# First projections on x times the norm's gains, the reciprocal root applied behind them

## The chip, the core and the metric

The kernel runs on one core of a Trainium2 chip. The metric is the device time of one execution in microseconds (us), with all data in the chip's memory at the start and the result there at the end. Of several runs the median is taken.

Five engines take part, each working through its own instructions in order: TensorE (PE in the profile, with its weight loads as PEld), VectorE (DVE), ScalarE (ACT), GpSimd (POOL) and SyncE (SP), which issues most of the DMAs. They wait for each other through semaphores only.

## The reference

The program is a two-layer encoder trunk over 256 tokens of 1024 values. The start of a layer, which is all that the change touches, is this (shortened):

```python
def rms_norm(x, g):
    y = x * rsqrt(mean(x * x, axis=-1) + 1e-6)
    return y * g

u = rms_norm(h, g_mix_pre)            # h is x in layer 0
z = u @ w_in                          # one wide projection, cut into:
#  GLA q | GLA k | GLA v | out-gate gg | decay ranks | GQA q | GQA k | GQA v | gate A | gate B
# GQA: q and k get a per-head RMSNorm (eps 1e-6) and rotary positions, then attention
# GLA: gated linear attention over chunks with decays made from the ranks; gates by sigmoids
# then merge, output projection, residual; SwiGLU FFN; per-layer input embedding
```

The reciprocal root is one number per token, so `(x * g) @ w` scaled by it afterwards is the same function.

## The kernel before

**Precision.** Every fp32 product is made of three passes over values rounded for TensorE. An operand t is split into a high part (ACT copies it to the rounded type) and a low part (DVE subtracts the high part from t). The three passes are high times high, low of x times high of the weights, high of x times low of the weights. In the names, `wh_` and `wl_` are the weights' parts, `raw_` the weights as loaded, `big_start` (uT in the code) the transposed x.

**Staging.** Tokens are two halves, hf 0 and hf 1, of 128. Weights come in units through a stream `ws`: a unit is a DMA of about 1 MB into one of a few raw tiles, two casts on ACT and two subtractions on DVE (`ws.pieces()` hands out the two pieces). The projections follow one another on PE: rq (the decay ranks and GQA's q, columns cut in three by `RQ`, 288, 384 and 384 wide), kv (GQA's k and v), gqk (GLA's q and k), v, gg, then the gates. Rq takes four units of two 128-row blocks each; its order is written out in `STEPS_FIRST` (half 0 and half 1 of unit 0, then of unit 1, and so on), with 6 accumulators of PSUM, one for each half and column block. `rq_first` writes out unit 0 pass by pass.

**Order by hand at the start.** `on(engine, f, ...)` (line 142) chains what is issued through it on its engine in the order in which the program says it; `start()` is a generator that says it, and the projection advances it by `tick()`. In the generator: squares of a half (`square` on ACT, `square_here` on DVE), the reciprocal root on POOL (`rstd`), `normed` (DVE multiplies x by the root), `turned` (PE transposes 128x128 blocks; gains applied on the way out of PSUM while splitting, column by column, or for four columns at once by one DVE multiplication of 512 columns ahead of the split). `warm_up(n)` issues matmuls on constants into a PSUM tile that nobody reads; `WARM` gives their numbers at three places. `grow` is the row of gains as loaded, `gcol` the same turned to a column by `gains()`.

**Behind the projections.** `put_q` (lines around 940) takes each accumulator of rq when its last unit is done: for the first column block `put_ranks` copies the decay ranks (POOL memsets a tile, three DVE copies), then `head_ss` squares each head on ACT with its sum, `inv_sqrt` makes the reciprocal roots on POOL in two instructions, and `rope` multiplies on DVE. `keys` does the same for kv. Behind gqk ACT copies four accumulators of 128x512 (lines 1124 and 1126). Where `tc.high_priority` stands, the scheduler moves the instructions ahead in their queues; `EMPTY_FIRST`, 1600, is the amount for layer 0's `put_q`, `EMPTY`, 100, for `keys`.

```python
with tc.high_priority(EMPTY if l else EMPTY_FIRST):
    if b == 0:
        ranks.append(Task(put_ranks(o, hf), part[0]))
    ...
    head_ss(src, n, dst, ss[:, hd : hd + n])
    inv_sqrt(ss[:, hd : hd + n], n, 1.0, P * EPS)
    rope(src, n, ropes[0], hf, dst)
```

## Time and profile before

| what | value |
|---|---|
| runs of before | 923.92, 924.27, 924.66 us |
| median | 924.27 us |
| span of the profiled execution | 922.9 us |
| median less that span | 1.4 us |
| PE busy | 912.2 us, 99% of the span |
| DVE busy | 786.1 us, 85% |
| ACT busy | 578.5 us, 63% |
| POOL busy | 83.8 us, 9% |
| first product of rq, of kv, of gqk | 7.92, 36.43, 47.56 us |

The profiled execution has no time of its own beside its span; the span runs from the first to the last instruction, and 1.4 us lie around it when it is set against the median. In the rows of the timeline the columns are start, length, engine, line, operation, output and inputs, shape, and how many instructions the row stands for; in brackets stands how long the engine idled before and what ended the wait. Lines that several instructions go through (120 and 104 for matmuls, 128 and 132 for splits, 142 for all of the start) are helpers: there the names of the tiles tell the rows apart. In the chain of waits the columns are start, length and what; "issue" is time in which the engine waited for nothing that the profile shows.

### The profile page before, as it was taken

Reading aid. Unit: us, or ns where it says so; the run is one execution under the profiler, and the core shown is the slowest. Engines: PE = TensorE matmul, PEld = TensorE weight load, DVE = VectorE, ACT = ScalarE, POOL = GpSimd, SP = SyncE. Lnnn points to the kernel's source line nnn. Section 1 sums busy time; section 2 is a strip of 40 time slices with the busy share of each in tenths; the row PEclk is TensorE's granted clock in tenths of the full one; section 3 lists DMA queues with packets and bytes.
Section 4 is the critical chain, followed back from the end, with each engine's and each line's share of the span. In section 5 each row is a group of like instructions: output and inputs, shape, how many; then the busy total and the mean of one; then the engine's idle time right before and its main releaser. Section 6 shows DMA issues by size and latency. Waiting matters only on the chain.

```text
span 922.9 us, 12406 instructions
## 1 busy us (share of the span) xinstructions
PE 912.2 (99%) x4668; PEld 776.2 (84%) x4668; DVE 786.1 (85%) x1002; ACT 578.5 (63%) x954; POOL 83.8 (9%) x147
## 2 busy tenths in 40 slices
PE   9999999999999999999999999999999999999996
PEld 6898888888888888888899988888888888888885
DVE  6898989987579998999779789798875799989884
ACT  4669676664567656566676677765644766565563
POOL 3400211300000000000114001100001000000000
PEclk9999999999999999999999999999999999999999
DMA  7463455656286565647576424454573756545361
GB/s 260 144 230 134 148 173 188 201 193 232 90 277 222 178 233 168 265 128 268 188 256 220 153 92 137 137 191 174 195 260 104 268 177 204 223 177 217 126 239 45
DMA packets 88679, 173.44 MB, mean 188 GB/s; under 512 B 3422, under 2 KB 26470, under 8 KB 88108
## 3 DMA queue, kind: packets, MB, share of 16 engines
q1 hardware_dynamic: 88460, 172.40, 54.0%
q8 instruction: 36, 0.59, 0.3%
q10 hardware_dynamic: 160, 0.27, 0.1%
q14 instruction: 23, 0.19, 0.1%
HBM read 169.50 MB, written 3.15 MB: 187 GB/s over the span
## 4 chain that ended last, share of the span: by engine, by line
PE 94%; DVE 2%; ACT 1%; DMA 1%; issue 1%; POOL 0%; POOLq 0%; DVEq 0%; ACTq 0%; SPq 0%
PE acc_0ffnin L120 12%; PE acc_1ffnin L120 11%; PE acc_1gate L120 7%; PE acc_0gate L120 7%; PE acc_0ffnin L104 7%; PE acc_1ffnin L104 7%; PE acc_1rq L120 3%; PE acc_0gqk L120 2%; PE acc_0wout L120 2%; PE acc_1gqk L120 2%; PE acc_1ple L120 2%; PE acc_0ple L120 2%; PE acc_0gg L120 2%; PE acc_1gg L120 2%; PE acc_0v L120 2%; PE acc_1merge L120 2%
## 5 line engine op out<-in xcount | busy, mean ns | idle before, releaser
L104 PE MATMUL acc_0ffnin<-wh_0ffnin,big_0ffnin 128*128 128x512 f32 x176 | 56.9, 393 | 0.0
L104 PE MATMUL acc_1ffnin<-wh_1ffnin,big_1ffnin 128*128 128x512 f32 x176 | 56.8, 392 | 0.0
L132 ACT CAST wh_1ffnin<-raw_1ffnin 128x1024 fp32r<-128x1024 f32 x38 | 38.5, 1049 | 27.3 <-DMA raw_1ffnin<-in_w_ffn_out_dram 8.7
L132 ACT CAST wh_0ffnin<-raw_0ffnin 128x1024 fp32r<-128x1024 f32 x38 | 38.4, 1048 | 23.8 <-PE acc_0ffnin L120 7.8
L128 DVE TENSOR_TENSOR wl_1ffnin<-raw_1ffnin,wh_1ffnin 128x1024 fp32r<-128x1024 f32 x38 | 45.0, 1221 | 8.9 <-ACT wh_1ffnin L132 8.9
L128 DVE TENSOR_TENSOR wl_0ffnin<-raw_0ffnin,wh_0ffnin 128x1024 fp32r<-128x1024 f32 x38 | 44.8, 1220 | 7.1 <-ACT wh_0ffnin L132 7.0
L120 PE MATMUL acc_1ffnin<-wh_1ffnin,big_1wout 128*128 128x512 f32 x168 | 42.5, 393 | 0.0
L120 PE MATMUL acc_0ffnin<-wh_0ffnin,big_0wout 128*128 128x512 f32 x168 | 42.5, 393 | 0.0
L104 PEld LDWEIGHTS acc_0ffnin<-wh_0ffnin,big_0ffnin 128*128 128x128 f32 x176 | 33.0, 188 | 7.1 <-DVE big_0ffnin L128 0.5
L104 PEld LDWEIGHTS acc_1ffnin<-wh_1ffnin,big_1ffnin 128*128 128x128 f32 x176 | 33.1, 188 | 6.7
L128 DVE TENSOR_TENSOR wl_1ffnin<-lent_1ffnin,wh_1ffnin 128x1024 fp32r<-128x1024 f32 x30 | 35.8, 1218 | 1.7 <-ACT wh_1ffnin L132 1.7
L128 DVE TENSOR_TENSOR wl_0ffnin<-lent_0ffnin,wh_0ffnin 128x1024 fp32r<-128x1024 f32 x30 | 35.8, 1216 | 1.7 <-ACT wh_0ffnin L132 1.7
L120 PEld LDWEIGHTS acc_1ffnin<-wh_1ffnin,big_1wout 128*128 128x128 f32 x168 | 31.1, 188 | 6.2
L120 PEld LDWEIGHTS acc_0ffnin<-wh_0ffnin,big_0wout 128*128 128x128 f32 x168 | 31.1, 188 | 6.2
L132 ACT CAST wh_1ffnin<-lent_1ffnin 128x1024 fp32r<-128x1024 f32 x30 | 30.7, 1053 | 7.1 <-PE acc_1ffnin L104 3.9
L132 ACT CAST wh_0ffnin<-lent_0ffnin 128x1024 fp32r<-128x1024 f32 x30 | 30.7, 1054 | 6.7 <-PE acc_0ffnin L104 3.9
L104 PE MATMUL acc_0ffnin<-wl_0ffnin,big_0ffnin 128*128 128x512 f32 x88 | 34.3, 389 | 0.0
L104 PE MATMUL acc_1ffnin<-wl_1ffnin,big_1ffnin 128*128 128x512 f32 x88 | 34.3, 389 | 0.0
L128 DVE TENSOR_TENSOR wl_1gate<-raw_1gate,wh_1gate 128x1024 fp32r<-128x1024 f32 x20 | 23.6, 1219 | 5.4 <-ACT wh_1gate L132 5.3
L128 DVE TENSOR_TENSOR wl_0gate<-raw_0gate,wh_0gate 128x1024 fp32r<-128x1024 f32 x20 | 23.7, 1226 | 4.8 <-ACT wh_0gate L132 4.8
L132 ACT CAST wh_0gate<-raw_0gate 128x1024 fp32r<-128x1024 f32 x20 | 20.0, 1048 | 11.7 <-DMA raw_0gate<-in_w_o_attn_dram 5.6
L132 ACT CAST wh_1gate<-raw_1gate 128x1024 fp32r<-128x1024 f32 x20 | 20.0, 1049 | 11.5 <-DMA raw_1gate<-in_w_o_attn_dram 5.5
(695 smaller groups left out, 2691.8 us busy)
## 6 DMA issues: line engine op xcount, KB each, us to landing
raw_0ffnin<-in_w_ffn_out_dram SPq DMA_DIRECT2D x11, 1024.0 KB, 6.6
raw_1ffnin<-in_w_ffn_out_dram SPq DMA_DIRECT2D x11, 1024.0 KB, 5.1
lent_0ffnin<-in_w_ffn_in_dram SPq DMA_DIRECT2D x6, 1024.0 KB, 7.4
lent_1ffnin<-in_w_ffn_in_dram SPq DMA_DIRECT2D x6, 1024.0 KB, 8.3
raw_0v<-in_w_in_dram SPq DMA_DIRECT2D x4, 1024.0 KB, 4.9
raw_0gate<-in_w_o_gla_dram SPq DMA_DIRECT2D x4, 1024.0 KB, 4.9
raw_0gate<-in_w_o_attn_dram SPq DMA_DIRECT2D x4, 1024.0 KB, 5.1
raw_0wout<-in_w_ffn_in_dram SPq DMA_DIRECT2D x8, 512.0 KB, 4.9
```

Of the source, the lines that this page charges most:

```text
L104: return nc.tensor.matmul(o, lhsT, rhs, start=start, stop=stop)
L120: nc.tensor.matmul(o, x, y, start=start and n == 0, stop=stop and n == len(seq) - 1, **kw)
L128: nc.vector.tensor_tensor(out=out, in0=in0, in1=in1, op=ALU.subtract)
L132: nc.scalar.copy(hi, src)
```

## The change

Norm and projection change places in layer 0. x is transposed as it lands; its gains are applied during the split, its reciprocal root `rs` behind each projection: as the scale of the squares in `head_ss`, as one more POOL multiplication behind `inv_sqrt`'s two instructions (`by`), in `put_ranks`, in the splits of v and of the values of kv (`split_by`), in the copies of gg and in the sigmoids of the gates. Gqk's accumulators have tokens along the free axis, so the roots are needed as a row there: `spread_rows` makes it (two diagonals on DVE, two matmuls against ones on PE, one ACT copy), emitted right behind the keys, and the four evictions of gqk move from ACT to DVE, which multiplies by that row.

The left 512 columns of both halves are loaded first, each on a queue of its own; the right columns follow the first weights. `rq_first` takes both halves' blocks in turn. The squares and roots move behind unit 1, the rotary tables (`rope_tables`) into `start()`, ahead of the decay's weights (`up_weights`). The warming matmuls become 6 of 128 columns (on `seed`, written by POOL), 6 and 3 of 512 columns. Unchanged lines are mostly left out, and the body of the removed `turned`.

```diff
--- before.py
+++ after.py
...
 RQ = ((0, 288), (288, 672), (672, 1056))
-WARM = 7, 3, 1
+WARM = 6, 6, 3
...
             line[e] = f(*args, **kw)
+    seed = cp.tile([P, P], BF16, tag="seed", name="seed")
+    on("pool", nc.gpsimd.memset, seed, 1.0)
...
     grow = mid()[0:8, 0:P]
-    def load_x(hf, queues=(("dma", nc.sync), ("dma", nc.sync))):
-        for j, (e, q) in enumerate(queues):
-            c = slice(j * 512, (j + 1) * 512)
-            on(e, q.dma_start, h[:, hf, c], a["x"][0, hf * P : (hf + 1) * P, c])
-    load_x(0, (("dma", nc.sync), ("act", nc.scalar)))
+    def load_x(hf, j, e="dma", q=nc.sync):
+        c = slice(j * 512, (j + 1) * 512)
+        on(e, q.dma_start, h[:, hf, c], a["x"][0, hf * P : (hf + 1) * P, c])
+    load_x(0, 0)
+    load_x(1, 0, "act", nc.scalar)
+    on("act", nc.scalar.dma_start, grow, a["g_mix_pre"][0].rearrange("(k p) -> k p", p=P))
...
         return tc.issue_after(last_pow[0].ins) if last_pow[0] is not None else nullcontext()
-    def inv_sqrt(t, n, mul, add):
+    def inv_sqrt(t, n, mul, add, by=None):
...
         last_pow[0] = nc.gpsimd.tensor_tensor(out=t, in0=t, in1=neghalf[:, :n], op=ALU.pow)
+        if by is not None:
+            with in_turn():
+                last_pow[0] = nc.gpsimd.tensor_scalar(out=t, in0=t, scalar1=by, scalar2=None, op0=ALU.mult)
+    def split_by(hi, lo, src, r):
+        if r is None:
+            return split(hi, lo, src)
+        nc.scalar.activation(hi, src, AF.Copy, bias=0.0, scale=r)
+        nc.vector.scalar_tensor_tensor(
+            out=lo, in0=src, scalar=r, in1=hi.bitcast(F32), op0=ALU.mult, op1=ALU.subtract
+        )
...
         return wup
-    x1 = [lambda: load_x(1)]
-    on("act", nc.scalar.dma_start, grow, a["g_mix_pre"][0].rearrange("(k p) -> k p", p=P))
-    ws.load(lambda: x1 and x1.pop()())
     ws.load()
+    ws.load()
+    load_x(0, 1)
+    load_x(1, 1)
...
     gcol = small(8, "gcol", 1)
-    def warm_up(n):
+    def warm_up(n, wide=False):
+        x = keep if wide else seed
         for _ in range(n):
-            on("pe", mm, warm, keep[:, 0:P], keep, True, True)
+            on("pe", mm, warm[:, 0 : x.shape[-1]], seed, x, True, True)
     warm_up(WARM[0])
+    warm_up(WARM[1], True)
     uT = Split()
-    ss, rs, xn = [small(2, "ss") for _ in range(2)], [small(1, "rstd") for _ in range(2)], [mid(), mid()]
+    ss = [small(2, "ss") for _ in range(2)]
+    rs, ropes_first = [small(1, "rs", 2) for _ in range(2)], []
...
         last_pow[0] = line["pool"]
-    def normed(hf, k, n):
-        c = slice(k * P, (k + n) * P)
-        on("dve", nc.vector.tensor_scalar, out=xn[hf][:, c], in0=h[:, hf, c], scalar1=rs[hf], scalar2=None, op0=ALU.mult)
     def gains():
...
         on("dve", nc.vector.tensor_copy, gcol, ps[:, 0:8])
+    def low(hi, lo, src):
+        on("dve", nc.vector.tensor_tensor, out=lo, in0=src, in1=hi.bitcast(F32), op=ALU.subtract)
     def split_here(hi, lo, src):
         on("act", nc.scalar.copy, hi, src)
-        on("dve", nc.vector.tensor_tensor, out=lo, in0=src, in1=hi.bitcast(F32), op=ALU.subtract)
-    def turned(hf, k, n):
...
+        low(hi, lo, src)
+    banks = {}
+    def turn(hf, *ks):
+        if (hf, ks[0] // 4) not in banks:
+            banks[hf, ks[0] // 4] = aux()
+        for k in ks:
+            ps = banks[hf, k // 4][:, k % 4 * P : (k % 4 + 1) * P]
+            on("pe", nc.tensor.transpose, ps, h[:, hf, k * P : (k + 1) * P], ident)
+    def high(hf, *ks):
+        for k in ks:
+            ps = banks[hf, k // 4][:, k % 4 * P : (k % 4 + 1) * P]
+            on("act", nc.scalar.activation, uT.at(k, 1, hf * P, P)[0][:, 0, :], ps, AF.Copy, bias=0.0, scale=gcol[:, k : k + 1])
+    def rest(hf, *ks):
+        for k in ks:
+            ps = banks[hf, k // 4][:, k % 4 * P : (k % 4 + 1) * P]
+            hi, lo = (t[:, 0, :] for t in uT.at(k, 1, hf * P, P))
+            on("dve", nc.vector.scalar_tensor_tensor, out=lo, in0=ps, scalar=gcol[:, k : k + 1],
+               in1=hi.bitcast(F32), op0=ALU.mult, op1=ALU.subtract)
     def start():
         cut = lambda piece, c: [t[:, c] for t in piece]
-        def low(hi, lo, src):
-            on("dve", nc.vector.tensor_tensor, out=lo, in0=src, in1=hi.bitcast(F32), op=ALU.subtract)
-        first, rest = cut(unit_a, slice(0, 288)), cut(unit_a, slice(288, 1056))
-        square(0, 0)
-        square_here(0, 1)
         gains()
-        warm_up(WARM[1])
-        rstd(0)
-        on("act", nc.scalar.copy, unit_a[0], unit_a[2])
-        normed(0, 0, 2)
-        low(*first)
-        turned(0, 0, 2)
-        warm_up(WARM[2])
-        square(1, 0)
-        square_here(1, 1)
-        rstd(1)
-        low(*rest)
-        normed(1, 0, 2)
-        split_here(*unit_b)
+        turn(0, 0)
+        turn(1, 0)
+        turn(0, 1)
+        turn(1, 1)
+        turn(0, 2, 3)
+        warm_up(WARM[2], True)
+        high(0, 0)
+        high(1, 0)
+        for c in RQ:
+            on("act", nc.scalar.copy, *(t[:, slice(*c)] for t in unit_a[::2]))
+        rest(0, 0)
+        rest(1, 0)
+        low(*cut(unit_a, slice(0, 288)))
+        high(0, 1)
+        high(1, 1)
+        low(*cut(unit_a, slice(288, 1056)))
+        on("act", nc.scalar.copy, unit_b[0], unit_b[2])
+        rest(0, 1)
+        rest(1, 1)
+        high(0, 2, 3)
+        low(*unit_b)
+        rest(0, 2, 3)
...
         yield 2
-        turned(1, 0, 2)
-        normed(0, 2, 2)
-        normed(1, 2, 2)
-        yield 3
+        turn(1, 2, 3)
+        high(1, 2, 3)
+        rest(1, 2, 3)
+        yield 4
         split_here(*unit_c)
-        turned(0, 2, 2)
         split_here(*unit_d)
-        turned(1, 2, 2)
...
         for hf in range(2):
-            normed(hf, 4, 4)
+            square(hf, 0)
         yield 2
+        turn(0, 4, 5, 6, 7)
+        for hf in range(2):
+            square_here(hf, 1)
+            rstd(hf)
+        ropes_first.extend(rope_tables(0))
+        high(0, 4, 5, 6, 7)
+        rest(0, 4, 5, 6, 7)
+        yield 1
+        turn(1, 4, 5, 6, 7)
+        high(1, 4, 5, 6, 7)
+        rest(1, 4, 5, 6, 7)
...
         ws.fill()
-        yield WAIT_FIRST
+    def spread_rows():
+        both = mid()
+        diag, ones, out = both[:, 0:T], both[:, T : T + P], both[:, 512 : 512 + T]
+        nc.gpsimd.memset(ones, 1.0)
+        ps = aux()
         for hf in range(2):
-            turned(hf, 4, 4)
+            s = slice(hf * P, (hf + 1) * P)
+            nc.vector.tensor_scalar(out=diag[:, s], in0=ident, scalar1=rs[hf], scalar2=None, op0=ALU.mult)
+            mm(ps[:, s], ones, diag[:, s], True, True)
+        nc.scalar.copy(out, ps[:, 0:T])
+        return out
     def keep_embedding():
...
         part[0] = f"{l}rq"
+        rows = [None, None] if l else rs
...
         if l == 0:
+            ropes = ropes_first
             with after_start:
-                ropes = rope_tables(0)
-            wup = up_weights(0)
+                wup = up_weights(0)
...
             nc.vector.tensor_tensor(out=hv(dst), in0=hv(dst), in1=hv(t2), op=ALU.add)
-        def head_ss(src, n, junk, ss):
+        def head_ss(src, n, junk, ss, hf):
+            by = {} if rows[hf] is None else {"scale": rows[hf]}
...
                 s = slice(i * P, (i + 1) * P)
-                nc.scalar.activation(junk[:, s], src[:, s], AF.Square, accum_out=ss[:, i : i + 1])
+                nc.scalar.activation(junk[:, s], src[:, s], AF.Square, accum_out=ss[:, i : i + 1], **by)
         def put_ranks(o, hf):
...
             with tc.high_priority(EMPTY):
-                nc.vector.tensor_copy(r[:, :, 0:16].bitcast(F32R), src)
-                vsub(r[:, :, 32:48].bitcast(F32R), src, r[:, :, 0:16])
+                if rows[hf] is None:
+                    nc.vector.tensor_copy(r[:, :, 0:16].bitcast(F32R), src)
+                    vsub(r[:, :, 32:48].bitcast(F32R), src, r[:, :, 0:16])
+                else:
+                    nc.vector.tensor_scalar(
+                        out=r[:, :, 0:16].bitcast(F32R), in0=src, scalar1=rows[hf], scalar2=None, op0=ALU.mult
+                    )
+                    nc.vector.scalar_tensor_tensor(
+                        out=r[:, :, 32:48].bitcast(F32R), in0=src, scalar=rows[hf], in1=r[:, :, 0:16],
+                        op0=ALU.mult, op1=ALU.subtract,
+                    )
...
             yield W["r"]
...
                 src, dst = o[:, lo : c1 - c0], qr[:, hd * P : (hd + n) * P]
-                head_ss(src, n, dst, ss[:, hd : hd + n])
-                inv_sqrt(ss[:, hd : hd + n], n, 1.0, P * EPS)
+                head_ss(src, n, dst, ss[:, hd : hd + n], hf)
+                inv_sqrt(ss[:, hd : hd + n], n, 1.0, P * EPS, rows[hf])
...
         def rq_step(o, hf, b, u):
...
             tick()
-        def rq_first(os_, hf):
-            uT.need(hf)
-            orders = (((0, 0, 2),), ((0, 1), (1, 0)), ((1, 2, 1),)), (((0, 0, 2),), ((1, 0, 2),), ((0, 1), (1, 1)))
-            for step in orders[hf]:
-                for k, *ps in step:
+        def rq_first(os_):
+            for k in range(2):
+                for hf, ps in ((0, (0, 2)), (1, (0, 2)), (0, (1,)), (1, (1,))):
...
                             x, y = ((ah, h), (ah, lo), (al, h))[p]
-                            mm(os_[b][:, : c1 - c0], x, y, k + p == 0, False)
-                tick()
+                            mm(os_[hf, b][:, : c1 - c0], x, y, k + p == 0, False)
+                    tick()
...
                 rq_step(o[hf, b], hf, b, u)
-            elif b == 2:
-                rq_first([o[hf, i] for i in range(3)], hf)
+            elif (hf, b) == (1, 2):
+                rq_first(o)
...
                     ss = small(2, "kss")
-                    head_ss(o[hf], 2, kr, ss)
-                    inv_sqrt(ss, 2, 1.0 / P, EPS)
+                    head_ss(o[hf], 2, kr, ss, hf)
+                    inv_sqrt(ss, 2, 1.0 / P, EPS, rows[hf])
...
                     s = slice(hf * 256, (hf + 1) * 256)
-                    split(avh[:, s], avl[:, s], o[hf][:, 256:512])
+                    split_by(avh[:, s], avl[:, s], o[hf][:, 256:512], rows[hf])
...
         keys = Task(keys(project(uT)), f"{l}kv")
+        if l == 0:
+            spread = spread_rows()
...
                 src = o[i].rearrange("p (h t) -> p h t", t=T)
-                if x == 0:
+                if l == 0:
+                    nc.vector.scalar_tensor_tensor(
+                        out=dst, in0=src, scalar=1.0 if x else P**-0.5,
+                        in1=spread.unsqueeze(1).broadcast_to([P, 2, T]), op0=ALU.mult, op1=ALU.mult,
+                    )
+                elif x == 0:
...
             for hf, o in enumerate(project(uT)):
-                split(*(t[:, hf, j * 512 : (j + 1) * 512] for t in v), o)
+                split_by(*(t[:, hf, j * 512 : (j + 1) * 512] for t in v), o, rows[hf])
...
             for hf in range(2):
-                nc.scalar.copy(gg[:, hf, j * 512 : (j + 1) * 512], o[hf])
+                dst = gg[:, hf, j * 512 : (j + 1) * 512]
+                if rows[hf] is None:
+                    nc.scalar.copy(dst, o[hf])
+                else:
+                    nc.scalar.activation(dst, o[hf], AF.Copy, bias=0.0, scale=rows[hf])
...
         def out_gate():
...
             with tc.issue_after(last_exp[0].ins):
-                nc.scalar.activation(sgate[br][:, hf, j * 512 : (j + 1) * 512], src, AF.Sigmoid)
+                by = {} if rows[hf] is None else {"scale": rows[hf]}
+                nc.scalar.activation(sgate[br][:, hf, j * 512 : (j + 1) * 512], src, AF.Sigmoid, **by)
         def blocks(sp, then):
```

More of the change, by code (lines that the diff above doesn't have):

```diff
@@ L767, in gains @@
         on("dve", nc.vector.tensor_copy, gcol, ps[:, 0:8])
+    def low(hi, lo, src):
+        on("dve", nc.vector.tensor_tensor, out=lo, in0=src, in1=hi.bitcast(F32), op=ALU.subtract)
     def split_here(hi, lo, src):
         on("act", nc.scalar.copy, hi, src)
-        on("dve", nc.vector.tensor_tensor, out=lo, in0=src, in1=hi.bitcast(F32), op=ALU.subtract)
-    def turned(hf, k, n):
-        ps = aux()
-        for i in range(n):
-            on("pe", nc.tensor.transpose, ps[:, i * P : (i + 1) * P], xn[hf][:, (k + i) * P : (k + i + 1) * P], ident)
-        hi, lo = uT.at(k, n, hf * P, P)
-        if n == 4:
-            y = t512()
-            on("dve", nc.vector.tensor_tensor, out=y.rearrange("p (k t) -> p k t", t=P),
-               in0=ps.rearrange("p (k t) -> p k t", t=P), in1=gcol[:, k : k + n].unsqueeze(2).broadcast_to([P, n, P]), op=ALU.mult)
-            split_here(hi, lo, y.rearrange("p (k t) -> p k t", t=P))
-            return
-        for i in range(n):
-            on("act", nc.scalar.activation, hi[:, i, :], ps[:, i * P : (i + 1) * P], AF.Copy, bias=0.0,
-               scale=gcol[:, k + i : k + i + 1])
-        for i in range(n):
-            on("dve", nc.vector.scalar_tensor_tensor, out=lo[:, i, :], in0=ps[:, i * P : (i + 1) * P],
-               scalar=gcol[:, k + i : k + i + 1], in1=hi[:, i, :].bitcast(F32), op0=ALU.mult, op1=ALU.subtract)
```

## The prediction

> **What bounds the kernel now.** I read the page's totals and its chain of waits first (whose idle time costs anything), then the chain of the first 50 us in order of time, then each engine's timeline there, because most of what the change touches lies ahead of 80 us.
>
> ```profile
> span 922.9 us, 12406 instructions
> PE 912.2 (99%) x4668; PEld 776.2 (84%) x4668; DVE 786.1 (85%) x1002; ACT 578.5 (63%) x954; POOL 83.8 (9%) x147
> PE 94%; DVE 2%; ACT 1%; DMA 1%; issue 1%; POOL 0%; POOLq 0%; DVEq 0%; ACTq 0%; SPq 0%
> ```
>
> TensorE is the bound: PE holds 94% of the chain. Time can be won where PE is not yet fed, and lost where a product waits for an operand. The chain of the first 50 us (start, length, what):
>
> ```profile
> 18.88 1.32 DVE mid_start L142 x2
> 20.20 2.59 DVE wl_start L142 x2
> 22.79 0.61 DVE t_start L142
> ...
> 24.09 12.12 PE acc_0rq L120 x72
> 36.21 0.22 PE aux_0rq L934 x2
> 36.43 4.09 PE acc_0kv L120 x18
> ...
> 40.74 6.82 PE acc_0kv L120 x30
> 47.56 2.51 PE acc_0gqk L120 x21
> ```
>
> The first projection, rq (four units of weights, 36 matmuls each), is held once by a DVE queue that normalises x, splits weights and multiplies by gains (18.88 to 23.40). Kv's 48 matmuls begin at 36.43, gqk's at 47.56. I sum to that point: behind it both kernels run the same matmuls.
>
> **The change part by part. Start.** PE's timeline of before (start, length, what, idle before it in brackets):
>
> ```profile
> 1.65 3.17 PE L104 MATMUL warm<-keep 128*128 128x512 bf16 x7 [1.65 <-DVE keep L142]
> 4.75 0.27 PE L142 MATMUL aux_start<-ident,mid_start 8*128 8x8 f32 x1
> 6.78 0.69 PE L142 MATMUL aux_start<-ident,mid_start 128*128 128x128 f32 x2 [0.36 <-DVE mid_start L142]
> 7.26 0.63 PE L104 MATMUL warm<-keep 128*128 128x512 bf16 x1
> 7.92 2.13 PE L104 MATMUL acc_0rq<-wh_start,big_start 128*128 128x288 f32 x6
> 9.85 0.44 PE L104 MATMUL acc_0rq<-wl_start,big_start 128*128 128x288 f32 x1
> 11.06 0.51 PE L104 MATMUL acc_0rq<-wh_start,big_start 128*128 128x384 f32 x2
> 21.38 1.03 PE L142 MATMUL aux_start<-ident,mid_start 128*128 128x128 f32 x8
> 24.09 1.40 PE L120 MATMUL acc_0rq<-wh_start,big_start 128*128 128x288 f32 x6 [0.63 <-ACT big_start L142]
> ```
>
> DVE and ACT beside it:
>
> ```profile
> 4.50 0.69 DVE L142 SCALAR_TENSOR_TENSOR t_start<-h 128x512 f32<-128x512 f32 x1 [2.91 <-DMA h<-in_x_dram]
> 5.73 1.07 ACT L142 CAST wh_start<-raw_start 128x1056 fp32r<-128x1056 f32 x1 [0.68 <-DMA raw_start<-in_w_in_dram]
> 7.50 0.62 ACT L142 ACTIVATE big_start<-aux_start,gcol_start 128x128 fp32r<-128x128 f32 x2 [0.70 <-PE aux_start L142]
> ```
>
> What goes ahead of the first product is the square, the reciprocal root and the normalising of x (4.50 to 6.78). The transposes now take x as it lands. Both left halves of x stand first on two queues, as the two pieces of half 0 did, so I let them land at 4.5 as those did. From there: gains 0.27, six transposes at 0.24 (the pair at 6.78 lies 0.48 ahead of its follower) 1.44, three wide warming matmuls at 3.17/7 = 0.45 1.36: 7.6. ACT meanwhile has the weights from 5.73 on, and needs two splits (0.62) and 288 of 1056 columns (0.29): no later. Drains overlap in part, so I take 7.4, ends 7.2 and 7.9, against 7.92: **0.5 us won**.
>
> *Pace.* Six first matmuls take 1.93 us (7.92 to 9.85), 0.32 each; later 72 take 12.12, 0.17 each. The pace doubles between 9.85 and 11.06 (I use 10.8), though the page's granted clock is full throughout. The trace of before can't show when it doubles in the changed kernel. Ends: already by 7.4, or at 10.8 as here, which costs (10.8−7.4)/2 = 1.7. Nearest rows, by stretches (span; PE, PEld, DVE, ACT, POOL busy; clock, DMA share, GB/s):
>
> ```profile
> 4.00:8.00 4.00, 3.60 (x10) 0.96 (x8) 1.59 (x5) 2.29 (x5) 0.87 (x2) 1.00 1.03 399
> 8.00:12.00 4.00, 4.00 (x17) 3.73 (x17) 2.99 (x7) 1.72 (x5) 1.43 (x2) 1.00 0.75 281
> 28.00:32.00 4.00, 4.00 (x27) 4.00 (x26) 1.68 (x2) 1.88 (x2) 0.00 (x0) 1.00 0.29 71
> 48.00:76.00 28.00, 28.00 (x238) 28.00 (x237) 24.73 (x49) 21.59 (x43) 1.10 (x3) 1.00 0.69 243
> ```
>
> With PE idle 0.40 between 4 and 8 the pace did not rise by 8; in 8 to 12 it was busy throughout, and the pace rose. The changed kernel's PE is busy earlier, from about 1 us (a POOL memset of a small seed in place of the DVE's keep), and idles about 0.3 while gains are fetched at 4.5. That lies between the two, so the ends are nearly even; I take the early one, since here PE also works through the stretch before (in before it began at 1.65), and its idle time is one piece.
>
> The Trainium skill, "TensorE: Matmul & The Clock Gate", Part 1 (The HAM clock gate), says that the clock doubles after one busy free-running window of about 3.4 us, whose phase varies. By that rule, with a boundary at 10.8, the one before lies near 7.4, the early end; the trace agrees in the doubling and can't show another run's phase.
>
> *Rq.* 144 matmuls at 0.164 ((12.12−0.30)/72; a wait of 0.30 for the second half's split lies in that piece) are 23.6; ten later transposes at 0.13 are 1.3. The waits at 24.09 and behind it go, 0.93 in all: the DVE queue loses the two `normed` (1.32) and the two multiplications (0.61 each), and ACT has its splits one at a time. Next late is the low part of unit 1's weights, by up to 0.3; I cost it at nothing. The ropes' POOL work and the squares run beside PE. Kv starts at 7.4+23.6+1.3+0.2 = 32.5 (early), or 34.2 (late), instead of 36.43: **3.9 or 2.2 us won**.
>
> *Kv: given back.* Here the order of the queues matters. Rows of before around it, DVE, ACT and POOL:
>
> ```profile
> 32.01 0.19 DVE L928 CAST t_0rq<-acc_0rq 128x32 fp32r<-128x32 f32 x1 [2.34 <-PE acc_0rq L120]
> 32.43 2.35 DVE L128 TENSOR_TENSOR wl_start<-raw_start,wh_start 128x1024 fp32r<-128x1024 f32 x2
> 38.80 1.35 DVE L125 TENSOR_TENSOR mid_0rq<-acc_0rq,rope_0rq 128x384 f32<-128x384 f32 x3
> 40.07 0.88 DVE L125 TENSOR_TENSOR t_0rq<-acc_0rq,rope_0rq 128x256 f32<-128x256 f32 x2
> 40.86 0.89 DVE L911 TENSOR_TENSOR mid_0rq<-mid_0rq,t_0rq 128x256 f32<-128x256 f32 x2
> ```
>
> ```profile
> 25.93 3.95 ACT L132 CAST wh_start<-raw_start 128x1056 fp32r<-128x1056 f32 x4
> 32.52 0.28 ACT L916 ACTIVATE mid_0rq<-acc_0rq 128x128 f32<-128x128 f32 x1 [2.64 <-DVE t_0rq L930]
> 37.01 2.01 ACT L132 CAST wh_0rq<-raw_start 128x1024 fp32r<-128x1024 f32 x2
> 35.44 0.20 POOL L454 TENSOR_SCALAR qss_0rq<-qss_0rq 128x3 f32<-128x3 f32 x1
> 35.72 0.86 POOL L455 TENSOR_TENSOR qss_0rq<-qss_0rq,neghalf 128x3 f32<-128x3 f32 x1
> 37.74 0.26 POOL L923 MEMSET t_0rq<- 128x192 f32 x1
> ```
>
> Before, both high parts of kv's first unit are cast by 29.9 and both low parts by 34.8, ahead of the rope multiplications. In the changed kernel's instruction order the second cast stands on ACT behind the squares of half 1's last accumulator, and both low parts on DVE behind nearly all rope work of q. Those squares wait for that accumulator's rank copies on DVE, these for a POOL memset, and this stands behind three reciprocal roots, each now with one more multiply. Counting from kv's start K: the first accumulator is ready at K−4.4 (32.01 against 36.43), its squares at K−3.9; three roots of 0.20+0.86+0.20 and three gaps of 0.08 each are 4.5, the memsets 0.5: K+1.1; ranks and two squares 0.8, cast 1.0: K+2.9. PE's first eight products need only the first cast: 0.2+8×0.227 (6.82/30) = K+2.0. **Wait 0.9 to 1.3.** The second eight end near K+5. DVE, from K+1.1: ranks and a sum 0.9, eight rope operations (rows 38.80 to 40.86 and one more) 3.5, low part 1.2: K+6.7, **wait 1.2 to 1.6**; four products 0.9, while DVE does one more sum 0.46 and the second low part 1.2: **wait 0.7**. Together 2.8 to 3.6, taken as 3.2. The multiply adds 3×0.28 of this, the order the rest. Were the casts in time it would be nothing (a rival).
>
> *Spread row.* Two 128x128 products in full precision stand on PE between kv and gqk. No row shows one; transposes of that size take 0.13 to 0.24 each, so the two 0.25 to 0.5, taken 0.4 (0.9 if a full-precision product costs twice a transpose). Their diagonals (DVE) and ones (POOL) are made during kv.
>
> *Behind kv.* Scales in ACT's squares, copies and sigmoids replace scale-free forms of the same shape; v's splits stay one ACT and one DVE operation. Four evictions of gqk (128x512) go from ACT to DVE; the nearest DVE row is 22.79, 0.61 in the chain. DVE has 3.27 idle of 28 between 48 and 76, and 4×0.68 = 2.7 to add, while it holds 2% of the chain: it fits, narrowly. Taken 0, ends 0 and 2.7.
>
> *Sum at gqk's start.* Early: 32.5−36.43+3.2+0.4 = −0.3. Late: +1.4. The profiled span of 922.9 lies 1.4 below the median of 924.27 (time around the span, the same in both kernels), so 924.0 and 925.7.
>
> **Rivals.** (1) *Late doubling*: the sum above with the pace of before, 925.7. For it: the idle 0.3 at 4.5 is little less than the 0.40 that didn't do. (2) *Gain kept*: if POOL's roots or the casts come soon enough that kv doesn't wait, −0.3−3.2 or +1.4−3.2, about 921–922.5. Against it: ACT and DVE execute in order, and ACT had idle time there before, so the place in the queue decides. (3) *Slower, DVE as bound behind kv*: with the evictions DVE has 27.4 us of work in 28, and the rope work it postponed arrives there. It decides once the idle 3.27 is mostly bound to waits for PE or ACT; then up to 2.7 falls on gqk's weights' low parts: 926.0 (with half of it, on the late sum 927) to 926.7. For it: DVE's 85% over the whole span; against: its 2% of the chain. (4) *The start doesn't move*: the first product needs the cast weights too, and if these, not x, are last (the cast of 5.73 was done by 6.8, its low part by 7.3), the first product stays at 7.9 and the early sum is 924.5: no change either.
>
> **How the numbers follow.** Forecast, early doubling with kv's waits: 0.45, 924.0. Late doubling: 0.28. Gain kept: 0.13. DVE bound: 0.12. The start unmoved: 0.02. A difference under 0.2%, 1.85 us, is about what a measurement can't tell from none. Faster by more: gain kept, and a tail of the early case (waits at 2.0 instead of 3.2): 0.18. Slower by more: DVE bound, and the upper third of the late case: 0.22. Same: 0.60. The range from 921.8 to 926.9 takes in the early and late sums with 2.8 to 3.6 of waits, most of rival 2, and rival 3 but for its end. The forecast's own: 923 to 925.
>
> **What would show it.** First real product at 7.2 to 7.6 and a pace of 0.16 from there on or from about 10.8; no PE idle between 8 and 32; kv's first product at 32 to 34.3; three PE waits inside kv, the first released by ACT's cast, two by DVE's low parts, 2.8 to 3.6 together; gqk at 47 to 49; no PE idle from there to 80. It is wrong if kv runs without waits (then it is faster), or if PE idles between 48 and 80 for DVE (then slower).

## The result, and the profile after

| | before | changed |
|---|---|---|
| median of 13 runs each, us | 924.74 | 926.70 |
| lowest and highest, us | 923.92, 925.88 | 925.96, 927.50 |
| span of the profiled execution, us | 922.9 | 924.1 |

The ratio is 1.0022, with a 95% interval of 1.0014 to 1.0030: slower by 2 us, 0.2%. The span of the changed kernel's profiled execution is 0.5 us under the median span of its runs (924.6; before's is at its median, 922.9), and its runs have 2.06 us around the span where before's have 1.73. So the profile shows 1.2 of the 1.96 us.

The page's first line, PE's row and the chain by engine, of the changed kernel:

```profile
span 924.1 us, 12442 instructions
PE 911.3 (99%) x4676; PEld 776.6 (84%) x4676; DVE 785.4 (85%) x1006; ACT 580.7 (63%) x959; POOL 88.5 (10%) x157
PE 93%; DVE 2%; ACT 1%; issue 1%; POOL 1%; DMA 1%; POOLq 0%; DVEq 0%; ACTq 0%; SPq 0%
```

Nothing stands out there; POOL has come from 0% to 1% of the chain. The place shows in PE's timeline (start, length, what, idle before):

```profile
1.04 0.82 PE L104 MATMUL warm<-seed 128*128 128x128 bf16 x6 [1.04 <-POOL seed L142]
4.56 1.20 PE L142 MATMUL aux_start<-ident,h 128*128 128x128 f32 x6
5.60 0.81 PE L104 MATMUL warm<-keep,seed 128*128 128x512 bf16 x3
6.80 2.40 PE L104 MATMUL acc_0rq<-wh_start,big_start 128*128 128x288 f32 x12 [0.39 <-ACT wh_start L142]
9.04 0.29 PE L104 MATMUL acc_0rq<-wl_start,big_start 128*128 128x288 f32 x1
...
31.88 2.14 PE L120 MATMUL acc_0kv<-wh_start,big_start 128*128 128x512 f32 x8
35.14 0.42 PE L987 MATMUL aux_0rq<-ident,t_0rq 128*81 128x128 f32 x2 [1.12 <-DVE t_0rq L983]
36.73 2.14 PE L120 MATMUL acc_0kv<-wh_start,big_start 128*128 128x512 f32 x8 [1.18 <-ACT wh_start L132]
39.50 1.19 PE L120 MATMUL acc_0kv<-wl_start,big_start 128*128 128x512 f32 x4 [0.63 <-DVE wl_start L128]
41.10 1.21 PE L120 MATMUL acc_0kv<-wl_start,big_start 128*128 128x512 f32 x4 [0.42 <-DVE wl_start L128]
...
47.63 0.61 PE L104 MATMUL aux_0kv<-mid_0kv 128*128 128x128 f32 x4
47.99 1.20 PE L120 MATMUL acc_0gqk<-big_start,wh_0rq 128*128 128x256 f32 x8
```

The start does what it was to do. The first product begins at 6.80, twelve take 2.24 us (0.19 each, so the pace has already doubled), there is no wait up to kv, and kv begins at 31.88 instead of 36.18. Then PE waits four times inside kv. From kv's first product to gqk's it takes 16.1 us, where before took 11.2 (36.18 to 47.40): 4.9 more, of which 0.36 are the spread row's products. 4.3 won, 4.9 lost: gqk begins 0.6 us later than before. Gqk itself takes another 0.6 more, as the chain shows at its start:

```profile
47.63 0.68 DVE wl_0rq L128
48.31 0.46 issue
48.77 1.23 DVE wl_0rq L128
50.00 0.04 issue
50.04 2.90 PE acc_0gqk L120 x22
```

A low part of gqk's first weights is made only at 48.77, since DVE comes late out of kv: ahead of these rows the same chain runs over k's squares on ACT, POOL's root for them (46.00 to 47.41) and DVE's multiplication by it.

The four waits are 3.35 us together, but PE loses 4.5 by them, since every restart adds some. Set against the pace of before (1.91 us from eight products' start to what follows them), 2.8 of it lie at the first two waits, up to the start of kv's second group of eight products, 0.9 at the third and 0.8 at the fourth.

What the queues did, in the changed kernel's timelines of DVE, POOL and ACT:

```profile
27.34 0.25 DVE L976 TENSOR_SCALAR t_0rq<-acc_0rq,rs_start 128x32 fp32r<-128x32 f32 x1 [2.49 <-PE acc_0rq L120]
34.03 0.25 DVE L976 TENSOR_SCALAR t_0rq<-acc_0rq,rs_start 128x32 fp32r<-128x32 f32 x1 [1.59 <-POOL t_0rq L967]
38.23 1.22 DVE L128 TENSOR_TENSOR wl_start<-raw_start,wh_start 128x1024 fp32r<-128x1024 f32 x1
39.83 1.22 DVE L128 TENSOR_TENSOR wl_start<-raw_start,wh_start 128x1024 fp32r<-128x1024 f32 x1
```

```profile
28.89 0.19 POOL L457 TENSOR_SCALAR qss_0rq<-qss_0rq 128x2 f32<-128x2 f32 x1 [1.49 <-ACT mid_0rq L960]
31.63 0.52 POOL L461 TENSOR_SCALAR qss_0rq<-qss_0rq,rs_start 128x3 f32<-128x3 f32 x1
33.48 0.31 POOL L461 TENSOR_SCALAR qss_0rq<-qss_0rq,rs_start 128x3 f32<-128x3 f32 x1
33.73 0.26 POOL L967 MEMSET t_0rq<- 128x192 f32 x1
```

```profile
27.99 0.37 ACT L960 ACTIVATE mid_0rq<-acc_0rq,rs_start 128x128 f32<-128x128 f32 x1 [5.24 <-DVE t_0rq L983]
30.74 1.08 ACT L132 CAST wh_start<-raw_start 128x1024 fp32r<-128x1024 f32 x1
34.94 0.37 ACT L960 ACTIVATE mid_0rq<-acc_0rq,rs_start 128x128 f32<-128x128 f32 x1 [1.01 <-DVE t_0rq L979]
35.64 1.04 ACT L132 CAST wh_start<-raw_start 128x1024 fp32r<-128x1024 f32 x1
```

The three roots occupy POOL from 28.89 to 33.79; the memset follows at 33.73, half 1's rank copies at 34.03, the last squares at 34.94, and only then comes kv's second cast, at 35.64, though ACT was idle for 5.24 us up to 27.99 and the data had landed by 26.3 at the latest (issued at 19.81; 5.1 to 6.5 us from issue to landing). The low parts begin at 38.23, behind q's rope work.

### The profile page after: what moved, and what is told of

The parts are those of the page before. It is cut to its first block, busy times and chain, and to the rows that moved or that the text cites. A ratio compares the mean times of both kernels' runs of the same rounds, so it can differ in the third digit from the quotient of the medians.

```text
span 924.1 us, 12442 instructions
## 1 busy us (share of the span) xinstructions
PE 911.3 (99%) x4676; PEld 776.6 (84%) x4676; DVE 785.4 (85%) x1006; ACT 580.7 (63%) x959; POOL 88.5 (10%) x157
## 4 chain that ended last, share of the span: by engine, by line
PE 93%; DVE 2%; ACT 1%; issue 1%; POOL 1%; DMA 1%; POOLq 0%; DVEq 0%; ACTq 0%; SPq 0%
PE acc_0ffnin L120 12%; PE acc_1ffnin L120 11%; PE acc_1gate L120 7%; PE acc_0gate L120 7%; PE acc_0ffnin L104 7%; PE acc_1ffnin L104 6%; PE acc_1rq L120 3%; PE acc_0wout L120 2%; PE acc_1gqk L120 2%; PE acc_1ple L120 2%; PE acc_0ple L120 2%; PE acc_1gg L120 2%; PE acc_0gg L120 2%; PE acc_0v L120 2%; PE acc_0merge L120 2%; PE acc_1merge L120 2%
## 5 line engine op out<-in xcount | busy, mean ns | idle before, releaser
L132 ACT CAST wh_1gate<-raw_1gate 128x1024 fp32r<-128x1024 f32 x20 | 20.0, 1049 | 11.7 <-DMA raw_1gate<-in_w_o_attn_dram 5.6
```

Source lines behind the costliest of these rows:

```text
L132: nc.scalar.copy(hi, src)
```

## The experiments

Three theories are set against each other: A, the places of kv's casts and low parts in the queues give the gain back; B, the spread row and gqk's evictions on DVE do; C, POOL's longer roots do. All times are medians. The kernels ran on several chips, each beside runs of before with medians of 924.6 to 925.0, so the ratio is the fairer comparison where two times lie close. The first product of rq begins anywhere from 6.48 to 7.25 us in profiles whose start is the same, since the pace of PE doubles earlier in one execution than in another (at 4.0 to 7.0, see the last section), so a few tenths of any start time below are that. The table has what decides: the first products of kv, gqk and v in the profile, and the two stretches between.

| kernel | us | ratio to before (95%) | kv | gqk | v | kv to gqk | gqk to v |
|---|---|---|---|---|---|---|---|
| before | 924.74 | 1 | 36.2 | 47.4 | 76.0 | 11.2 | 28.6 |
| changed | 926.70 | 1.0022 (1.0014–1.0030) | 31.9 | 48.0 | 77.2 | 16.1 | 29.2 |
| e1 casts early | 922.79 | 0.9979 (0.9970–0.9988) | 31.5 | 44.4 | 73.0 | 12.9 | 28.5 |
| e2 ranks early | 924.93 | 1.0003 (0.9994–1.0012) | 31.6 | 46.0 | 75.3 | 14.4 | 29.3 |
| e3 no root multiply | 925.51 | 1.0005 (0.9996–1.0015) | 32.2 | 47.3 | 76.2 | 15.0 | 28.9 |
| e4 evictions on ACT | 926.67 | 1.0022 (1.0013–1.0031) | 31.5 | 47.2 | 76.3 | 15.7 | 29.1 |
| e5 casts and ranks | 922.90 | 0.9980 (0.9971–0.9989) | 31.5 | 43.2 | 73.1 | 11.7 | 29.9 |
| e6 e5, root in eps | 921.36 | 0.9965 (0.9952–0.9977) | 31.9 | 43.7 | 72.2 | 11.8 | 28.5 |
| e7 casts only | 938.17 | 1.0149 (1.0135–1.0163) | 32.0 | 58.9 | 88.8 | 26.9 | 29.9 |
| e8 no warming | 928.96 | 1.0047 (1.0033–1.0061) | 34.5 | 50.6 | 79.8 | 16.1 | 29.2 |
| e9 e6, evictions on ACT | 921.56 | 0.9964 (0.9951–0.9978) | 31.5 | 42.7 | 71.2 | 11.2 | 28.5 |
| e10 e6, three warming fewer | 922.16 | 0.9971 (0.9961–0.9982) | 33.2 | 45.0 | 73.5 | 11.8 | 28.5 |

**e1: the splits and the diagonals moved up.**

```diff
         ws.open = True
-        ws.fill()
+        with tc.high_priority(2400):
+            ws.fill()
...
         if l == 0:
-            spread = spread_rows()
+            with tc.high_priority(200):
+                spread = spread_rows()
```

> Changed kernel, with the splits of kv's first unit moved up in their queues (ahead of q's squares on ACT and q's rope work on DVE) and the spread row's diagonals moved up too; no work is added or taken away. Theory A (the place in the queue gives the gain back): PE's three waits inside kv (in the changed kernel from 33.7 to 41.1 us, 4.7 us more between kv's first product and gqk's than before) go; kv starts at 31.8 as now, gqk at about 31.8+11.1+0.4 = 43.3, some 4.5 us earlier than in the changed kernel and 4 earlier than before: 922.2 us, ratio to before about 0.997. Rival B (the spread row and gqk's evictions on DVE are the loss): kv's waits move into gqk, time within 0.5 us of the changed kernel. Rival C (POOL's longer roots are the loss, wherever the casts stand): the rank copies of half 1 still come late and PE waits on them, gain 1.5 at most.

Measured: 3.9 us faster than the changed kernel. DVE's and PE's timelines of e1:

```profile
29.89 2.35 DVE L128 TENSOR_TENSOR wl_start<-raw_start,wh_start 128x1024 fp32r<-128x1024 f32 x2
36.87 0.42 PE L988 MATMUL aux_0rq<-ident,t_0rq 128*81 128x128 f32 x2 [1.00 <-DVE t_0rq L984]
```

Three of the four waits are gone with no work taken away; one is left, 1.00 us for half 1's rank copies. Theory A holds. The 12.9 us instead of the 11.5 expected are that wait and the restart behind it.

**e2: rank tiles set at the start.**

```diff
+        if l == 0:
+            both = t512()
+            with tc.high_priority(0):
+                ranks_first = [rank_tile(both[:, i * 192 : (i + 1) * 192]) for i in range(2)]
...
-            r = t512()[:, 0:192].rearrange("p (d r) -> p d r", d=2)
-            nc.gpsimd.memset(r, 0.0)
-            for c in (16, 80):
-                nc.gpsimd.memset(r[:, :, c : c + 1], 1.0)
+            r = ranks_first[hf] if l == 0 else rank_tile()
```

(`rank_tile` holds the three lines that go.)

> Changed kernel, with both halves' rank tiles set to their constants on POOL at the start (one tile for both), so that half 1's rank copies no longer wait behind the three reciprocal roots (memset at 33.73, copies at 34.03 in the changed kernel). Theory A: ACT's last squares and the second cast behind them come up to 1.7 us earlier, so PE's first two waits in kv (1.12 and 1.18) shrink; the low parts on DVE still stand behind the rope work and move up by less. Gain about 1 us, 925.7. Rival B: no change. Rival C: as A, about 1 us.

Measured: 1.8 us faster than the changed kernel, more than expected. PE waits twice instead of four times, in e2's timeline:

```profile
35.29 2.12 PE L120 MATMUL acc_0kv<-wh_start,big_start 128*128 128x512 f32 x8 [1.40 <-ACT wh_start L132]
39.11 1.19 PE L120 MATMUL acc_0kv<-wl_start,big_start 128*128 128x512 f32 x4 [0.41 <-DVE wl_start L128]
```

So a small memset behind three roots carried 1.8 of the loss, through the rank copies, the squares and the cast that queue behind it.

**e3: no multiply behind the roots.**

```diff
-                inv_sqrt(ss[:, hd : hd + n], n, 1.0, P * EPS, rows[hf])
+                inv_sqrt(ss[:, hd : hd + n], n, 1.0, P * EPS)
...
-                    inv_sqrt(ss, 2, 1.0 / P, EPS, rows[hf])
+                    inv_sqrt(ss, 2, 1.0 / P, EPS)
```

> Changed kernel without the additional multiplication behind the reciprocal roots of q and k (so the root of x's mean square is left out of q's and k's scales). Theory A: three of these stand ahead of half 1's rank memset, 0.33+0.52+0.31 and three gaps of 0.09 = 1.4 us; the wait inside kv shrinks by 0.9 to 1.4 us, 925.3 to 925.8; the rest of the loss stays. Rival C (POOL's longer roots are the loss): at least 2 us, 924.7 or less. Rival B: nothing.

Measured: 1.2 us faster, inside A's range. POOL's added work is a part of the loss, the smaller one.

**e4: evictions back on ACT, no spread row.**

```diff
-                if l == 0:
-                    nc.vector.scalar_tensor_tensor(
...
-                elif x == 0:
+                if x == 0:
...
-        if l == 0:
-            spread = spread_rows()
```

> Changed kernel with gqk's four evictions on ACT as before, and without the spread row (so the root is left out of GLA's q and k). Theory A: the two products in full precision (0.36 on PE) go and little else: 0.4 to 0.7 us, 926.0 to 926.3. Rival B (spread row and evictions on DVE are the loss): 2 us or more, 924.7 or less, and gqk's end no later than before. Rival C: 0.4.

Measured: no change in the time. In the profile v begins 0.9 us earlier than in the changed kernel (0.4 of it already at kv's first product, ahead of anything that e4 changes) and layer 1's rq 0.6 earlier, but layer 1's kv 0.2 later. In e4's timeline PE waits there once more for DVE, which itself waits 1.25 us for a root from POOL, where it waits 0.85 in the changed kernel; why, the profile doesn't show:

```profile
477.08 1.32 PE L442 MATMUL aux_0ple<-ident,mid_0ple 128*128 128x128 f32 x8 [0.38 <-DVE mid_0ple L512]
```

By itself inconclusive; e9 repeats it where kv doesn't wait.

**e5: e1 and e2 together.**

> The moved-up splits and diagonals (e1) together with the rank tiles set at the start (e2). In e1 one wait stays in kv, 1.00 us (with the drains about 1.3 us of PE's time, kv's first product to gqk's 12.9 us against 11.5 of work), released by half 1's rank copies, which wait for the memset behind the roots. Theory A: that goes too, gqk starts 1.0 to 1.3 us earlier than in e1, 921.5 to 921.8. If the roots themselves were the loss (rival C), the time stays at e1's 922.8.

Measured: kv is 1.2 us shorter than in e1, as expected, but the time is the same. Gqk takes 1.4 us more. POOL's and DVE's timelines of e5:

```profile
37.55 0.30 POOL L461 TENSOR_SCALAR qss_0rq<-qss_0rq,rs_start 128x2 f32<-128x2 f32 x1
39.36 4.95 POOL L461 TENSOR_SCALAR qss_0rq<-qss_0rq,rs_start 128x3 f32<-128x3 f32 x1
49.09 0.30 POOL L461 TENSOR_SCALAR kss_0kv<-kss_0kv,rs_start 128x2 f32<-128x2 f32 x1
```

```profile
39.50 4.62 DVE L128 TENSOR_TENSOR wl_0rq<-raw_start,wh_0rq 128x1024 fp32r<-128x1024 f32 x4
49.42 0.68 DVE L1077 TENSOR_SCALAR t_0kv<-t_0kv,kss_0kv 128x128 f32<-128x128 f32 x3 [1.27 <-POOL kss_0kv L461]
```

A multiplication of 128x3, 0.3 elsewhere, lasts 4.95 us: it spans four low parts that DVE makes in a row, and ends when they do. K's roots then come late, DVE waits 1.27 for them, and low parts of gqk's weights behind it. The time is the one that C named, though not by the wait that it named.

**e6: the root folded into eps.** With m the mean square plus eps of x, r = m^(-1/2), and s the head's sum of squares without r: r·(r²s + e)^(-1/2) = (s + e·m)^(-1/2).

```diff
+        for t, by in ((eps_q, P * EPS), (eps_k, EPS)):
+            on("pool", nc.gpsimd.tensor_scalar, out=t[hf], in0=rs[hf], scalar1=by, scalar2=None, op0=ALU.mult)
...
-                inv_sqrt(ss[:, hd : hd + n], n, 1.0, P * EPS, rows[hf])
+                inv_sqrt(ss[:, hd : hd + n], n, 1.0, P * EPS if l else eps_q[hf])
```

(For k likewise; `head_ss` is without its scale again.)

> As e5, and the additional multiplications on POOL and the scale of ACT's squares are folded into the eps of q's and k's reciprocal roots (eps times the mean square, made once for each half on POOL at the start); the result is the same function. Theory A: once kv's operands are early, nobody on the path waits for POOL: within 0.5 us of e5. Rival C: 1 us or more below e5.

Measured: 1.5 us under e5, 3.3 under before, which is what C expected: with the casts in place POOL does lie on the path. Q's roots are done at 38.29, ahead of the four low parts (from 39.73), so nothing of POOL's stretches beside them and DVE no longer waits for k's roots. About 0.3 of the gain lies around the span (2.10 us in e5, 1.76 in e6, medians), not in it; and e6 also takes the scale out of ACT's squares, which isn't separated here. The list of PE's waits up to 120 us (total, times, longest) has two rows, both ahead of the first products:

```profile
PE warm L104 <- POOL seed L142: 1.0, 1, 1.0
PE acc_0rq L104 <- ACT wh_start L142: 0.2, 1, 0.2
```

**e7: the splits moved up, the diagonals not.** Only the first half of e1's edit.

> As e1, but the spread row's diagonals stay at the place that the order gives them, which here is on DVE behind half 0's rope work of k, both values' splits and four low parts of later weights, while PE has the two products right behind kv. Theory A (the place in a queue decides, not the work): PE waits at the spread row for DVE, whose queue ahead of the diagonals holds about 7 low parts (8.5 us) and k's rope work (4 us) from 38 us on; some of that runs beside kv, so the wait is 6 to 10 us: 929 to 933 us, slower than both. Rival B in its plain form (the spread row's work itself costs): as e1, 922.8.

Measured: 938.17, still slower than expected. One row of e7's timeline says why:

```profile
58.02 1.19 PE L104 MATMUL aux_0kv<-mid_0kv 128*128 128x128 f32 x4 [13.42 <-DVE mid_0kv L877]
```

Two DVE instructions of 0.2 us, placed behind k's rope work and four low parts, hold PE for 13.4 us. Of this DVE itself spends 3.2 waiting for k's roots from POOL, where one instruction of q's roots lasted 4.61 us (0.88 otherwise) and put k's behind it; the expectation had only DVE's work. From e7's DVE timeline:

```profile
50.18 0.29 DVE L1068 TENSOR_SCALAR t_0kv<-t_0kv,kss_0kv 128x128 f32<-128x128 f32 x1 [1.95 <-POOL kss_0kv L461]
51.74 0.68 DVE L1068 TENSOR_SCALAR t_0kv<-t_0kv,kss_0kv 128x128 f32<-128x128 f32 x3 [1.27 <-POOL kss_0kv L461]
```

In the changed kernel the order has the diagonals ahead of k's rope work (at 43.90, 47.63 on PE); moving the splits alone let them fall behind it.

**e8: no warming matmuls.** `WARM = 0, 0, 0`.

> Changed kernel without any of the 15 warming matmuls. The first product is held by ACT's split of gains and weights, so it stays at 6.5 to 6.8. The forecast's step on the pace: PE has worked less before it, the pace of 0.16 us a matmul comes later than 7.4, at 8 to 11, and each us of that costs half: 0.3 to 1.8 us, 927.0 to 928.5, with kv's first product at 32.1 to 33.6. If the warming matmuls did nothing for the pace, 926.7 and 31.8.

Measured: 2.3 us slower, a little above the range; kv begins 2.7 us later. PE's timeline of e8:

```profile
7.33 3.89 PE L104 MATMUL acc_0rq<-wh_start,big_start 128*128 128x288 f32 x12 [1.03 <-ACT wh_start L142]
11.01 0.77 PE L104 MATMUL acc_0rq<-wl_start,big_start 128*128 128x288 f32 x2
...
39.39 3.28 PE L120 MATMUL acc_0kv<-wh_start,big_start 128*128 128x512 f32 x8 [1.17 <-ACT wh_start L132]
```

Twelve products take 3.7 us instead of 2.2, and transposes and gains ahead of them 0.5 more. The trace records that PE's full clock was granted from 12.69 on, where the expectation had 8 to 11 and the changed kernel has 5.28. From the first product on 2.1 us are lost by it; a half of the stretch from 7.33 to 12.69, as the forecast's step has it, would be 2.7. Inside kv the clock falls to half once more, from 40.00 to 43.41, behind the waits of 1.15 and 1.17; the row of 39.39 shows it (3.28 us, where the same eight products take 2.14 in the changed kernel). It doesn't lengthen kv (16.1 in both), since PE then no longer waits for the two low parts.

**e9: e6 with the evictions on ACT, no spread row.** The edit of e4 on e6.

> e6 with gqk's four evictions on ACT and without the spread row (the root is left out of GLA's q and k). In e6 PE has no wait between its first product and 120 us, so what the spread row and the evictions on DVE cost can be read without kv's waits in the way. Theory A: only the two products' 0.44 us go, and gqk takes 28.5 us from its first product to v's as in e6 and before: 920.9 us. Rival B: DVE freed of 2.7 us moves gqk's or v's products too, 1 us or more, 920.4 or less, and gqk takes under 28 us.

Measured: the time of e6 (921.56). Kv is 0.5 shorter and gqk takes the same 28.5 us: evictions on DVE cost PE nothing there. The 0.5 does not show in the time: v begins 1.0 earlier than in e6 (0.5 of it ahead of the first product, where the kernels are the same), but gg only 0.4 earlier, and layer 1's kv 0.6 later, much as in e4.

**e10: e6 with `WARM = 6, 6, 0`.**

> e6 without the last three warming matmuls (the ones behind the six transposes). In e6 and the changed kernel the first product waits for ACT (0.16 to 0.39 us) behind them, and the pace had doubled by 5.6, so they hold nothing up and give nothing: within 0.5 us of e6, 921.4. If they are what keeps the pace up through the transposes and the wait, the pace drops at 6 to 7 and the time rises by up to 1.7 us.

Measured: 0.8 us slower than e6 by the medians, 0.0006 in the ratio, and the two intervals overlap: the time alone doesn't settle it. PE's timeline of e10, then of e7, which has the three:

```profile
4.75 1.54 PE L142 MATMUL aux_start<-ident,h 128*128 128x128 f32 x6
7.33 3.54 PE L104 MATMUL acc_0rq<-wh_start,big_start 128*128 128x288 f32 x12 [1.04 <-ACT wh_start L142]
10.71 0.47 PE L104 MATMUL acc_0rq<-wl_start,big_start 128*128 128x288 f32 x2
```

```profile
4.59 1.54 PE L142 MATMUL aux_start<-ident,h 128*128 128x128 f32 x6
5.93 1.34 PE L104 MATMUL warm<-keep,seed 128*128 128x512 bf16 x3
7.17 2.41 PE L104 MATMUL acc_0rq<-wh_start,big_start 128*128 128x288 f32 x12
```

Without them PE idles 1.04 us ahead of the products, which then go at the slow pace for most of 3.4 us; kv begins 1.3 us later than in e6. The pace had not doubled before that gap: in both rows the six transposes are as slow as in e8. The traces record the full clock from 10.33 on in e10 and from 6.98 on in e7. Its changes lie 3.41 us apart, or a multiple of that (see the last section), so e10 could have had it at 6.92, next to e7's instant; but there PE had been idle since 6.29, where in e7 the three matmuls were running. So they do hold the pace in an execution whose instant comes as late as that. Where it comes sooner, at 4.0 to 6.0 in most of these traces, the pace is there ahead of the gap; that they give nothing then, no run shows. I expected no effect, having taken the doubling by 5.6 from the changed kernel's one profile, and was wrong for this execution. It is the slowest of e10's eight (a span of 922.3 us against a median of 920.5), so a typical one loses less than it shows.

## Why the prediction was wrong

The forecast was 924.0, no change to speak of; the kernel became slower by 0.2%. The range held 926.7, at its upper end, by luck: that end stood there for a late doubling of the pace and for DVE as the bound behind kv, and neither came. The 2.0 us lie just past the 1.85 that it counted as no change. The forecast's first products of kv and gqk in before (36.43 and 47.56) are those of the chain; the timeline, used here for both kernels, has 36.18 and 47.40. Step by step:

- *Start, 0.5 us won at 7.4.* 6.80: 1.1 won. The transposes were quicker than the row of before (1.04 for six to their follower, 0.17 each, not 0.24), since the pace doubled among them. What the first product waits for is ACT (0.39), against the forecast's "no later": it begins 1.04 us behind the end of the six transposes in every run with this start.
- *Pace, early end.* Right, and the term that mattered for the late case: it doubled before the first product. By the Trainium skill's rule ("TensorE: Matmul & The Clock Gate", Part 1, one busy window of about 3.4 us) it could come from 1.04+3.4 = 4.4 on; the transposes of 4.56 show it here, those of e8, which has no warming, do not. The trace records the full clock from 5.28 on, and the nine traces of kernels with this start from anywhere between 4.03 (a little sooner than the rule gives) and 6.98: that it came early enough was sound, that it came among the transposes was luck.
- *Rq.* 32.5 forecast for kv's start, 31.9 measured; no wait between, as said. 4.3 us won instead of 3.9.
- *Kv: this step failed, in size.* The mechanism is the one described, second cast and low parts behind q's work on ACT, DVE and POOL, and e1 shows it by order alone. But it cost 4.9−0.36 = 4.5 us instead of 3.2, and the term that was too small is its first wait, the one for the second cast: 2.8 us (1.12 and 1.18 idle, the rest restarts) instead of 0.9 to 1.3; the two for the low parts came to 0.9 and 0.8, against 1.2 to 1.6 and 0.7. The cast ended at 36.68, K+4.8, not K+2.9. The sum let POOL's roots begin when the squares do, at K−3.9; the squares did begin there (27.99), but the roots only at 28.89, K−3.0, behind two squares of 0.37 each and the reading of their sums. The roots took 4.9 instead of 4.5, as the multiplies last 0.31 to 0.52, not 0.20. So half 1's rank copies began at 34.03, K+2.2, not K+1.1, and from there to the cast it took 1.6 us instead of 0.8, since on DVE a rope addition stands between the copies (34.19) and on ACT two squares behind them. (The Trainium skill, "ScalarE: Activation LUTs", section "What ACT_TABLE_LOAD costs", gives about 93 ns more for each operand of one value per partition in an ACT instruction, as the scale is; the rows agree, 0.37 against 0.28.) The transposes of half 1's ranks, which the sum did not have, stand on PE between the two groups of products and split this wait in two; the cast's end would have held PE as long without them.
- *Spread row, 0.4.* 0.36; 0.5 of kv's time by e9. *Behind kv, 0.* 0.6: not by the evictions (e9), but by DVE's delay out of kv, which goes with the waits (28.5 in e1 and in e6).
- *Sum.* −0.3 forecast at gqk's start, +0.6 measured; +1.2 at v's, where the forecast had the same −0.3. To this come 0.3 us around the span and a profiled execution 0.5 below its median. These 0.3 go with POOL's added multiplications: the time around the span is 1.76 to 1.84 us (medians) in e3, e6, e9 and e10, which have none, and 1.96 to 2.16 in all the others and the changed kernel. What makes it there, no run shows.
- *Rivals.* Late doubling: no. Start unmoved: no, 6.80. Gain kept: not in this kernel, but e6 is that case, and 921.36 lies in its price (921 to 922.5). DVE as bound behind kv by the evictions: no, by e9.

The sign of the change was lost in a sum of two terms of 4 to 5 us each, where the gain was read from rows within 0.4, and the loss from rows of a different order within 1.3.

## What to carry to other kernels

When an early stage gets faster, look at what each in-order queue holds ahead of the next stage's operands: the 4.3 us won at the start came back in kv because a cast, two subtractions and a memset had kept their places behind another stage's work, and moving them up, with nothing removed, turned +2.0 us into −1.9. Count a chain through queues instruction by instruction, the tiny ones too: a memset carried 1.8 us, two 0.2 us diagonals, with POOL's delay ahead of them, 13. And repair one place at a time with the whole path in view, since each wait that goes uncovers the next (e1, e5, e6, e7).

## What the runs showed of the hardware

POOL's small instructions last longer while DVE makes low parts, at most by a whole run of them: 4.95 us instead of 0.31 beside four in a row (e5), 4.61 instead of 0.88 beside three with a rope addition between them (e7), and in the changed kernel 1.87 instead of 0.87 at 38.29 and 2.02 instead of 0.31 at 40.26. Not always to the run's end: the one of 40.26 ends at 42.28, while DVE goes from low part to low part until 43.32. That it is DVE's work was not isolated by a kernel of its own. The Trainium skill, "SBUF — State Buffer", section "Who interferes with whom", says that a DVE operation with two inputs in that memory, as the low parts are, contends with a POOL instruction that reads it, through ports that one of them holds exclusively; the rows agree, and show POOL kept out over as many as four in a row.

PE's full clock is granted, and taken back, at instants of a grid of 3.41 us whose place differs from execution to execution. In e8 the clock stood at half for 3.41 us (40.00 to 43.41), after 27.31 us at full, eight times as long; in e7, behind the wait of 13.4 us, at half for 13.65, four times, after 40.96 at full, twelve times. The page's granted clock hides the slow start, since the record begins only with the first full clock: at 10.85 us in before, at 12.69 in e8, at 10.33 in e10, and at 5.28, 4.97, 4.31, 5.95, 4.03, 4.74, 6.43, 6.98 and 4.46 in the changed kernel, e1 to e7 and e9. So it seems to matter where a gap of PE falls. With the grid set by these records, e8's waits of 1.15 and 1.17 lie in one stretch of it (36.59 to 40.00), behind which the clock fell; in the changed kernel the grid, at 36.0, cuts through the second of its waits of 1.12 and 1.18, and the clock stayed. How much idle time a stretch may hold, these runs don't settle.
